# A thirteenth pair of input-projection weight tiles in the block-product stage, and six fewer dense pieces inside attention

## The chip, the cores and the metric

The kernel runs on one core of one Trainium2 chip. The metric is the device time of one execution in microseconds (us), and less is better. The core has five engines that run side by side, each through its own queue in order: PE (TensorE, matmuls and transposes), DVE (VectorE), ACT (ScalarE), POOL (GpSimd) and SP (which here only issues DMAs).

## What is computed

One layer of a hybrid encoder on 1024 prompt rows and 8 x 16 sample rows (1152 rows in all, width 1024). The projection `h @ w_in` has 4352 columns, that is 34 weight tiles of 128 columns, and it is computed for all 1152 rows. Its results feed two attentions, A (8 query heads on 2 key heads) and B (8 heads), and two gates:

```python
h = rmsnorm(x, g_pre_mix)
qa, ka, va, qb, kb, vb, ga, gb = project(h, w_in)        # h @ w_in, 34 tiles of 128 columns
oa = band attention of (qa, ka, va), 3 chunks of 64 keys, with sinks and a bias
ob = band attention of (qb, kb, vb), 9 chunks of 64 keys, with a bias
merged = sigmoid(ga) * (oa @ w_oa) + sigmoid(gb) * (ob @ w_ob)
x = x + rmsnorm(merged @ w_out, g_post_mix)
x = x + rmsnorm(conv_ffn(rmsnorm(x, g_pre_ffn)), g_post_ffn)
```

Every float32 product is made of three fp32r products (high part by high part, high by low, low by high).

## The kernel before

The work runs in stages: normalisation and block products of the input projection, attention, the output projections with the gates, the gated MLP, the down projection. The change touches the first two.

**Block products (lines 160 to 522).** The contraction is halved, the rows are halved, and two weight tiles (a "pair", list `pairs`, line 199) are done together as a 2 x 2 block product in seven products instead of eight. A product is 24 matmuls (4 k-tiles, 3 part products, two chunks of 256 and 320 columns; `chunk_product`, line 136). The first `NA` = 7 pairs have their first two products done early, while the right-hand factors are still being built (`Away`), and the remaining five products later (`head_back`, `tail`). The pairs from the eighth on do all seven in one go (`head`, `tail`). The result goes to DRAM (`in_dr`, one buffer for each weight tile).

**Attention (lines 524 to 914).** Eight units, each of two heads: units 0 to 3 are branch A, 4 to 7 are branch B. A unit has five steps: two prompt steps `p0`, `p1`, the sample step `s`, and `p2`, `p3`. A prompt step handles 256 query rows. It makes scores on PE into the pool `pss1` (2 tiles of two banks; names `s`, line 693), adds the bias and takes the maximum on DVE (line 696), takes the exponential on ACT (line 701), the reciprocal and the scaling on DVE (lines 714, 718). The next step transposes its result on PE into the pool `pst1` (2 banks; names `pt`, line 735), copies each transposed tile to SBUF (`pk`), in turn on ACT (line 739) and DVE (line 737), and multiplies with the values on PE (`o`, line 750). In branch B a row block sees up to 640 keys, in branch A up to 256. The raw q, k and v rows of a unit are loaded and split into high and low parts ahead of time (`k6h`, `k6l`, `q6h`, `q6l`; lines 587 to 591).

**Dense pieces.** The weight tiles that are in no pair are listed in `dense_tiles` (line 840). Each is done without the block scheme, as three pieces of 24 matmuls over 384 rows (`dense_pieces`, line 554; names `d`, lines 117 to 119). A piece is cut in four quanta of 6 matmuls. `pieces_per_unit` (line 865) says how many pieces each unit takes, and `spread` puts their quanta between the instructions of the unit's steps. They give PE work while DVE and ACT prepare the next transposes. Three pieces of the last tile stay for the end, around the last transposes. Each dense weight tile is split into high and low parts by ACT (line 101) and POOL (line 104).

Within these stages the queues are not fixed by hand: a scheduler places each engine's instructions by their order in the program and by when it takes them to be ready.

Of the kernel before, what the change touches and what calls it, by code (L numbers as in the profile page):

```python
# [52 lines left out]
def encoder_step(ctx, tc, x, w_in, w_o, w_out, w_upg, w_down, kc, vc, state_conv, conv_w, conv_b,  # L53
# [109 lines left out]
    with ExitStack() as ph:  # L163
# [32 lines left out]

        pairs = [(4, 5), (0, 1), (2, 3), (10, 14), (6, 7), (11, 15)] + [(18 + n, 26 + n) for n in range(6)]
        NA = 7  # L200
        a1_dr = [dram.tile([P, 2 * CW], F32, name=f"a1_dr{f}") for f in range(NA)]
        rf = {}
# [316 lines left out]
    with ExitStack() as ph:  # L519
# [112 lines left out]
        def fetch(u):  # L632

            un = units[u]
            if u < 4:
                if u == 0:
                    rows(4, "ka", k_done(shared_a, "a", ka_new, 896))
                rows(u, f"q{u}", q_done(un, u))
            else:
                p = u - 4  # L640
                rows(10 + p, f"k{u}", k_done(un, f"{u}", kb_new[p], 512))
                rows(6 + p, f"q{u}", q_done(un, u))
                rows(14 + p, f"v{u}", v_done(un, f"{u}", vb_new[p], 512))
# [193 lines left out]
            later.append(late)  # L837

        later = []
        dense_tiles = [12, 16, 8, 13, 17, 9, 24, 32, 25, 33]  # L840
        pieces = []
        for col in dense_tiles:
            pieces += dense_pieces(col)
# [18 lines left out]
                done = upto  # L862

        fetch(0)
        pieces_per_unit = [3, 3, 3, 3, 4, 4, 4, 3]
        prev = None
        for u in range(8):
            n = pieces_per_unit[u]
# [440 lines left out]
    with ExitStack() as ph:  # L1309
# [119 lines left out]
        def stepper(name, pairs, main, extra, start, extra_start, own=False):  # L1429

            ops = [p.operands(name, own) for p in pairs]
            side = {"p2": "s2", "p1": "s1", "p5": "s1", "p3": "s2"}.get(name)
            n = 2 * len(pairs)

            def step(i, j):
                p, (z, w) = pairs[i // 2], ops[i // 2]
                if j < 0:
                    three(extra, getattr(p, side), w, i % 2, slice(0, P), extra_start and i == 0, i == n - 1)
                else:
                    three(main[j], z, w, i % 2, slice(j * P, (j + 1) * P), start and i == 0, i == n - 1)  # L1440

            return step, n, ([-1] if side else []) + [0, 1, 2, 3]
# [50 lines left out]
        for g in range(2):  # L1493
            last = g == 1
            pairs = [Pair(g, q) for q in range(3)]
# [37 lines left out]
            p5, n, _ = stepper("p5", pairs, xb, ex, False, True)  # L1533
# [4 lines left out]
            p3, n, _ = stepper("p3", pairs, xb, ex, False, False, True)  # L1538
# [94 lines left out]
```

## Time and profile before

| | us |
|---|---|
| median of three runs | 1635.86 (1635.2 to 1637.76) |
| profiled execution | 1635.94 |
| its span, first to last instruction | 1634.1 |
| five full block heads, 185.20 to 296.26 | 111.06 |
| unit 4 (4 pieces) | 44.60 |
| unit 5 (4 pieces) | 43.08 |
| unit 6 (4 pieces) | 43.06 |
| unit 7 (3 pieces) | 38.14 |

1.84 us of the profiled execution lie outside its span. In a timeline, a row is: start, duration, engine, line, operation, output<-inputs, tile, count of merged instructions, and in brackets how long the engine stood idle before it and whom it waited for. In a table of stretches, each engine has its busy time and in parentheses its instructions; PEclk is the granted PE clock as a share of full speed.

### The profile page before, as it was taken

What the parts mean: (1) busy time and instruction counts of PE and PEld (TensorE: products, weight loads), DVE (VectorE), ACT (ScalarE), POOL (GpSimd) and SP (SyncE); (2) the same over time, 40 slices, a digit from 0 to 9 for tenths busy, and PEclk for the clock granted to TensorE, in tenths of its full rate; (3) what the DMA queues carried; (4) which work ended last, traced back from release to release, by engine and by line L of the source; (5) the groups of instructions that cost most, each with busy time, mean ns of one, the idle gap of its engine ahead of it and who ended that gap; (6) DMA issues with size and microseconds to landing.
All of it is one profiled execution on the core that took longest, in us unless ns stands there. A gap on an engine that the chain in (4) does not pass through costs nothing.

```text
span 1634.1 us, 27922 instructions
## 1 busy us (share of the span) xinstructions
PE 1593.4 (98%) x10891; PEld 1470.7 (90%) x10891; DVE 1099.4 (67%) x2045; ACT 728.7 (45%) x1429; POOL 212.1 (13%) x287
## 2 busy tenths in 40 slices
PE   8999999999999999999999999999999999999998
PEld 6999999878788889978899999999999998888886
DVE  6976544777676746444497866766666767955997
ACT  7521233566555444332374344444444445434252
POOL 1000000221110004410002212211112211000002
PEclk9999999999999999999999999999999999999999
DMA  7654321654443255342264321221221219053023
GB/s 282 205 183 150 111 103 67 222 174 152 152 157 102 67 184 195 119 161 90 78 189 136 117 80 57 82 81 67 82 69 67 81 49 367 1 204 124 1 78 154
DMA packets 93045, 205.94 MB, mean 126 GB/s; under 512 B 19321, under 2 KB 42793, under 8 KB 92914
## 3 DMA queue, kind: packets, MB, share of 16 engines
q1 hardware_dynamic: 92640, 203.35, 36.2%
q8 instruction: 85, 1.39, 0.4%
q0 software_dynamic: 272, 0.81, 0.1%
q14 instruction: 46, 0.38, 0.1%
q10 hardware_dynamic: 2, 0.00, 0.0%
HBM read 147.61 MB, written 61.24 MB: 128 GB/s over the span
## 4 chain that ended last, share of the span: by engine, by line
PE 86%; DVE 5%; ACT 3%; DMA 3%; issue 2%; POOL 1%; SPq 0%; DVEq 0%; POOLq 0%; ACTq 0%
PE x L143 16%; PE z L143 8%; PE x L1415 8%; PE ix L143 7%; PE p L1415 6%; PE iz L143 4%; PE y L143 4%; PE o L750 2%; PE d L117 2%; PE pt L735 2%; PE d L119 2%; PE r L1090 2%; PE mp L956 2%; PE mp L958 2%; PE mp L957 2%; PE d L118 2%
## 5 line engine op out<-in xcount | busy, mean ns | idle before, releaser
L143 PE MATMUL x<-xot,s 128*128 128x288 f32 x1152 | 157.7, 295 | 1.5 <-DVE w L1200 1.5
L143 PEld LDWEIGHTS x<-xot,s 128*128 128x128 f32 x1152 | 154.9, 188 | 1.7 <-ACT a L1049 1.7
L1415 PE MATMUL x<-wbp,zap 128*128 128x512 f32 x576 | 135.3, 389 | 0.0
L1415 PEld LDWEIGHTS x<-wbp,zap 128*128 128x128 f32 x576 | 108.1, 188 | 22.5
L1049 ACT ACTIVATE s<-uw 128x512 fp32r<-128x512 f32 x96 | 60.2, 627 | 94.8 <-issue 41.7
L1415 PE MATMUL p<-wbp,zap 128*128 128x512 f32 x432 | 100.5, 389 | 0.0
L701 ACT ACTIVATE p<-p,m 128x256 f32<-128x256 f32 (+4 forms) x128 | 74.8, 587 | 57.3 <-DVE m L696 57.2
L1415 PEld LDWEIGHTS p<-wbp,zap 128*128 128x128 f32 x432 | 81.1, 188 | 16.9
L1050 DVE TENSOR_TENSOR s<-uw,s 128x512 fp32r<-128x512 f32 x96 | 70.2, 731 | 33.8 <-ACT s L1049 33.7
L1241 DVE SCALAR_TENSOR_TENSOR wk<-w,cw,wk 128x128 f32<-128x128 f32 (+2 forms) x144 | 83.2, 614 | 6.7 <-ACT wk L1239 5.9
L1050 DVE TENSOR_TENSOR a<-uw,a 128x512 fp32r<-128x512 f32 x62 | 42.9, 693 | 63.4 <-ACT a L1049 62.2
L143 PE MATMUL x<-xob,s 128*128 128x288 f32 x576 | 81.1, 295 | 3.3 <-DVE wk L1200 3.3
L143 PEld LDWEIGHTS x<-xob,s 128*128 128x128 f32 x576 | 78.1, 188 | 3.9 <-ACT wk L1239 3.1
L143 PE MATMUL z<-xot,s 128*128 128x288 f32 x576 | 80.7, 295 | 0.0
L143 PE MATMUL z<-xot,a 128*128 128x288 f32 x576 | 80.7, 295 | 0.0
L143 PE MATMUL ix<-t,s_i 128*128 128x256 f32 (+1 forms) x576 | 78.4, 294 | 0.7 <-DVE iu L191 0.7
L143 PEld LDWEIGHTS z<-xot,s 128*128 128x128 f32 x576 | 78.1, 188 | 0.0
L143 PEld LDWEIGHTS z<-xot,a 128*128 128x128 f32 x576 | 78.1, 188 | 0.0
L143 PEld LDWEIGHTS ix<-t,s_i 128*128 128x128 f32 x576 | 76.8, 187 | 0.9 <-DVE iu L191 0.9
L176 ACT ACTIVATE s_i<-iw 128x512 fp32r<-128x512 f32 x48 | 30.1, 631 | 86.2 <-PE ix L143 38.1
L143 PE MATMUL x<-xob,a 128*128 128x288 f32 x456 | 63.9, 295 | 0.0
L143 PE MATMUL y<-xob,a 128*128 128x288 f32 x456 | 63.9, 295 | 0.0
(634 smaller groups left out, 3837.1 us busy)
## 6 DMA issues: line engine op xcount, KB each, us to landing
uw<-in_w_upg SPq DMA_DIRECT2D x53, 512.0 KB, 3.7
iw<-in_w_in SPq DMA_DIRECT2D x24, 512.0 KB, 3.7
gg<-in_dr SPq DMA_DIRECT2D x16, 576.0 KB, 4.1
z_dr<-wk SPq DMA_DIRECT2D x23, 256.0 KB, 2.1
in_dr<-gt SPq DMA_DIRECT2D x30, 192.0 KB, 1.9
z_dr<-wk SPq DMA_DIRECT2D x23, 224.0 KB, 1.9
xt<-in_x SPq DMA_DIRECT2D x9, 512.0 KB, 7.6
oT<-o_dr SPq DMA_DIRECT2D x8, 576.0 KB, 6.5
```

What stands on the lines that cost most here:

```text
L117: nc.tensor.matmul(ps, w[:, 0, a], xg[0][:, b], start=start and k == 0, stop=False)
L118: nc.tensor.matmul(ps, w[:, 0, a], xg[1][:, b], start=False, stop=False)
L119: nc.tensor.matmul(ps, w[:, 1, a], xg[0][:, b], start=False, stop=stop and k == nk - 1)
L143: nc.tensor.matmul(ps, w[:, i, k], right(j, c, k), start=first and n == 0, stop=last and n == len(todo) - 1, skip_group_check=True)
L701: nc.scalar.activation(p[h][:, 0:n], p[h][:, 0:n], AF.Exp, bias=least[h], scale=-1.0, accum_out=st.d[:, h, i:i + 1])
L735: nc.tensor.transpose(pt[:, h * nb + b], st.p[i][h][:, c:c + P], ident[:])
L750: nc.tensor.matmul(ps[r, c], k.vs[:, kb, r], p[h], start=n == 0, stop=n == len(st.pv) - 1)
L956: nc.tensor.matmul(ps[:], self.sp[:, 0, k], oT[k][:, 0, c], start=k % 4 == 0, stop=False)
L1049: nc.scalar.activation(sp[:, 0], src, AF.Copy)
L1050: nc.vector.tensor_tensor(sp[:, 1], src, fr(sp[:, 0]), op=ALU.subtract)
L1241: nc.vector.scalar_tensor_tensor(out, src(t), cw[:, f, t:t + 1], out, op0=ALU.mult, op1=ALU.add)
L1415: nc.tensor.matmul(ps, z[:, i, k, c], w[:, j, k], start=first and n == 0, stop=last and n == 2, skip_group_check=True)
```

## The change

Weight tiles 8 and 9 (the queries of units 6 and 7) leave the dense list and become the seventh pair. `NA` stays 7, so the pair (18, 26), which was the seventh, is now the first that does all its products in one go. The list of dense tiles goes from ten to eight, 30 pieces to 24, and the units' shares are set anew: the units of branch A keep three each, those of branch B go from 4, 4, 4, 3 to 2, 3, 2, 2, and three are left for the end as before.

```diff
-        pairs = [(4, 5), (0, 1), (2, 3), (10, 14), (6, 7), (11, 15)] + [(18 + n, 26 + n) for n in range(6)]
+        pairs = [(4, 5), (0, 1), (2, 3), (10, 14), (6, 7), (11, 15), (8, 9)] + [(18 + n, 26 + n) for n in range(6)]
...
-        dense_tiles = [12, 16, 8, 13, 17, 9, 24, 32, 25, 33]
+        dense_tiles = [12, 16, 13, 17, 24, 32, 25, 33]
...
-        pieces_per_unit = [3, 3, 3, 3, 4, 4, 4, 3]
+        pieces_per_unit = [3, 3, 3, 3, 2, 3, 2, 2]
```

On PE, at the end of the block products, before (x, y and z are the accumulators of a pair; `t_` and `xk_` are right-hand factors; each row is the 12 matmuls of one chunk; `w12s` is the first dense tile):

```order
L143 MATMUL ix_0_2964<-xk_129,s_i_3124 128x256 x12
L143 MATMUL ix_1_2965<-xk_129,s_i_3124 128x320 x12
L143 MATMUL iz_0_3028<-t_1038,a_i_3155 128x256 x12
L143 MATMUL iz_1_3029<-t_1038,a_i_3155 128x320 x12
L117 MATMUL d_0_3318<-xk_128,w12s 128x384
```

And after the change, from the same `iz_1_3029` on:

```order
L143 MATMUL iz_1_3029<-t_1038,a_i_3155 128x320 x12
L143 MATMUL ix_0_3188<-xk_128,a_i_3190 128x256 x12
L143 MATMUL ix_1_3189<-xk_128,a_i_3190 128x320 x12
L143 MATMUL iy_0_3220<-xk_129,a_i_3222 128x256 x12
L143 MATMUL iy_1_3221<-xk_129,a_i_3222 128x320 x12
L143 MATMUL iz_0_3252<-t_615,s_i_3255 128x256 x12
L143 MATMUL iz_1_3253<-t_615,s_i_3255 128x320 x12
L143 MATMUL ix_0_3188<-t_616,s_i_3283 128x256 x12
L143 MATMUL ix_1_3189<-t_616,s_i_3283 128x320 x12
L143 MATMUL ix_0_3188<-t_617,s_i_3314 128x256 x12
L143 MATMUL ix_1_3189<-t_617,s_i_3314 128x320 x12
```

Two more products (four rows) follow these before the first dense piece: one more full head stands at the end of the stage.

On PE in step p2 of unit 6, between the first and the second half of the scores, before (`ts` are the transposes of the sample step, `w32s` a dense tile):

```order
L807 MATMUL ts_6544<-ident,pm_3241 128x128
L806 MATMUL ts_6544<-ident,ps_6445 128x128
L807 MATMUL ts_6544<-ident,pm_3245 128x128
L117 MATMUL d_1_6551<-xk_128,w32s 128x384
L118 MATMUL d_1_6551<-xk_128,w32s 128x384
L119 MATMUL d_1_6551<-xk_128,w32s 128x384
```

And after:

```order
L807 MATMUL ts_6646<-ident,pm_3465 128x128
L806 MATMUL ts_6646<-ident,ps_6553 128x128
L807 MATMUL ts_6646<-ident,pm_3469 128x128
L693 MATMUL s_2_1_0_6655<-k6h,q6h 128x320 x2
L693 MATMUL s_2_1_0_6655<-k6h,q6l 128x320 x2
L693 MATMUL s_2_1_0_6655<-k6l,q6h 128x320 x2
L693 MATMUL s_2_1_1_6664<-k6h,q6h 128x320 x2
```

The quantum of six dense matmuls that stood between the two halves is gone, so the second half's scores follow at once; the twelve after the scores remain of eighteen.

On DVE at the end of unit 4, before (`m` and `p` of line 696 are the maxima and sums of the last scores, `k6l` and `q6l` the low parts of unit 6's rows, `oos` the sample output, `oo` the copy of the values' product):

```order
L696 ISA p_3_1_1_5521,m_3_5456<-s_3_1_1_5531,bt_1_5048,m_3_5456 128x320
L589 TENSOR_TENSOR k6l<-k6raw,k6h 128x512 x2
L737 COPY pk_2_5_5559<-pt_2_5_5558 128x256
L714 RECIPROCAL dn_3_5457<-dn_3_5457 128x4
L718 TENSOR_SCALAR p_3_0_0_5458<-p_3_0_0_5458,dn_3_5457 128x640
```

And after:

```order
L696 ISA p_3_1_1_5690,m_3_5637<-s_3_1_1_5700,bt_1_5272,m_3_5637 128x320
L589 TENSOR_TENSOR k6l<-k6raw,k6h 128x512 x2
L591 SCALAR_TENSOR_TENSOR q6l<-q6raw,q6h 128x512
L714 RECIPROCAL dn_3_5638<-dn_3_5638 128x4
L737 COPY pk_2_5_5728<-pt_2_5_5727 128x256
L718 TENSOR_SCALAR p_3_0_0_5639<-p_3_0_0_5639,dn_3_5638 128x640
```

One of the two halves of the split `q6l` now stands ahead of the reciprocal and the scaling of the last step; before, both stood behind them.

## The prediction

> **What bounds the kernel now.** I read the page first, then PE's timeline and the table of stretches for the two stages that the change touches, then DVE's timeline inside attention. From the page, the span, PE's busy time, and the chain of work that ended last, by engine:
>
> ```profile
> span 1634.1 us, 27922 instructions
> PE 1593.4 (98%) x10891; PEld 1470.7 (90%) x10891; DVE 1099.4 (67%) x2045; ACT 728.7 (45%) x1429; POOL 212.1 (13%) x287
> PE 86%; DVE 5%; ACT 3%; DMA 3%; issue 2%; POOL 1%; SPq 0%; DVEq 0%; POOLq 0%; ACTq 0%
> ```
>
> PE is the bound nearly everywhere: work taken from it counts, as long as it doesn't then stand waiting. Stretches of time (length, then busy time and instruction count of PE, PEld, DVE, ACT, POOL, then PE's clock and the DMA): the last five heads of the block products, unit 0, and units 4 to 7.
>
> ```profile
> 185.20:296.30 111.10, 111.10 (x843) 111.10 (x842) 47.47 (x82) 38.71 (x78) 7.83 (x16) 1.00 0.31 105
> 296.30:323.00 26.70, 25.89 (x221) 20.95 (x221) 21.49 (x80) 15.95 (x56) 2.40 (x5) 1.00 0.59 191
> ...
> 411.83:456.43 44.60, 41.61 (x346) 34.74 (x344) 33.28 (x104) 23.95 (x59) 7.54 (x9) 0.96 0.52 165
> 456.43:499.51 43.08, 42.80 (x370) 35.66 (x368) 30.75 (x104) 23.32 (x58) 5.60 (x8) 1.00 0.43 144
> 499.51:542.57 43.06, 42.78 (x371) 35.65 (x369) 28.80 (x100) 22.07 (x55) 3.20 (x2) 1.00 0.25 82
> 542.57:580.71 38.14, 37.94 (x337) 30.30 (x335) 27.88 (x99) 19.87 (x51) 1.72 (x1) 1.00 0.17 54
> ```
>
> In the heads PE has no gap and DVE is busy 43%. In units 5 to 7 PE has almost no gap either, but there that is the work of the dense pieces: DVE is already at 67% to 73%, and what PE does between two dense quanta waits on DVE and ACT.
>
> **The change, part by part.**
>
> *The added head.* The first product of a head starts at 185.20, the first of the next at 207.41, and the first dense matmul after five heads at 296.26:
>
> ```profile
> 185.20 3.33 PE L143 MATMUL ix<-xk,a_i 128*128 128x256 f32 x24
> 207.41 3.33 PE L143 MATMUL ix<-xk,a_i 128*128 128x256 f32 x24
> ...
> 296.26 0.34 PE L117 MATMUL d<-xk,w12s 128*128 128x384 f32 x1
> ```
>
> 111.06 / 5 = 22.21 us per head. Nothing hides an extra one, since PE has no gap there; it also loads two weight tiles and stores four results, beside DMA at 0.31 of its time. That (18, 26) loses its early start and (8, 9) gains it leaves seven early pairs. **+22.2.**
>
> *The six dense pieces.* Inside one piece:
>
> ```profile
> 580.99 0.34 PE L118 MATMUL d<-xk,w33s 128*128 128x384 f32 x1
> ...
> 584.98 1.03 PE L735 MATMUL pt<-ident,p 128*128 128x128 f32 x8
> ```
>
> 23 matmuls take 3.99 us, 0.1735 each, so a piece of 24 is 4.16 and six are 25.0: two from unit 4, one from unit 5, two from unit 6, one from unit 7. **-25.0** of PE work. The two weight splits and six copies to SBUF that go with them lay on ACT and POOL, beside PE: I count them as nothing.
>
> Without any new wait the sum is 22.2 - 25.0 = -2.8. What decides is how much of the 25.0 comes back as PE waiting in units 4 to 7.
>
> *The first piece taken from a unit* is in the trace already: unit 6 has four pieces and lasts 43.06, unit 7 three and 38.14. Unit 6 has also the transposes of unit 7's values:
>
> ```profile
> 513.96 0.66 PE L621 MATMUL vt<-ident,v7raw 128*128 128x128 f32 x4
> 514.88 0.66 PE L621 MATMUL vt<-ident,v7raw 128*128 128x128 f32 x4
> ```
>
> 43.06 - 38.14 - 1.32 = 3.6, so a piece of 4.16 bought 3.6, and 0.56 came back.
>
> *The second piece* isn't in the trace. The chains that it uncovers are, in unit 6. DVE after the first scores of p2, after the last, and in p3; PE at the start of each group of scores:
>
> ```profile
> 522.79 0.41 PE L693 MATMUL s<-k6h,q6h 64*128 64x320 f32 x2
> 525.51 0.42 PE L693 MATMUL s<-k6h,q6h 64*128 64x320 f32 x2
> 526.34 0.31 PE L693 MATMUL s<-k6l,q6h 64*128 64x320 f32 x2
> 530.93 0.42 PE L693 MATMUL s<-k6h,q6h 64*128 64x320 f32 x2
> ```
>
> ```profile
> 525.31 0.08 DVE L696 DVE_READ_ACCUMULATOR2_ANT m<- 128x1 f32 x1
> ...
> 528.19 0.09 DVE L696 DVE_READ_ACCUMULATOR2_ANT m<- 128x1 f32 x1
> 529.61 0.18 DVE L714 RECIPROCAL dn<-dn 128x4 f32<-128x4 f32 x1 [1.33 <-ACT p L701]
> 529.82 1.94 DVE L718 TENSOR_SCALAR p<-p,dn 128x640 f32<-128x640 f32 x4
> 531.69 0.49 DVE L696 CUSTOM_DVE_ANT_0 p<-s,bt 128x320 f32<-128x320 f32 x1
> ...
> 533.46 0.69 DVE L737 COPY pk<-pt 128x512 f32<-128x512 f32 x1
> ```
>
> (1) Scores have two tiles. DVE frees the second at 525.39, and PE wants it after 525.51: covered by one quantum (6 x 0.1735 = 1.04), which the change takes out there. PE would want it at about 524.9: a wait of 0.5. (2) From the end of the scores (526.65) to the end of the scaling (531.76) are 5.1 us, in which PE has dense work, the sample step's values and the next scores (530.93, about 1.1 long): 5.4 of cover. A quantum less leaves 4.35: a wait of 0.75. (3) In p3 the fourth transposed tile waits for DVE's copy of the second, which stands behind four maxima, until 533.46 + 0.69; PE had a quantum there, now none: about 0.5. Together 1.75 for a second piece; in p0 and p1 the copies and exponentials pace PE too, but the scheduler moved the next scores forward into those gaps, and I add nothing for them.
>
> *The splits on DVE.* One half of `q6l` now stands ahead of the last scaling of unit 4. Both halves of such a split take 1.29:
>
> ```profile
> 498.63 1.29 DVE L591 SCALAR_TENSOR_TENSOR q7l<-q7raw,q7h 128x512 fp32r<-128x512 f32 x2
> ```
>
> so half is 0.65, and the transposes of unit 5's p0, queued on PE behind that scaling, come later by it: 0.65.
>
> Returned: unit 4 0.56 + 1.75 = 2.3, unit 5 0.56, unit 6 2.3, unit 7 (its second piece) 1.75, the split 0.65: 7.6. **Sum: 22.2 - 25.0 + 7.6 = +4.8.** The profiled execution took 1635.94, and the median of the runs is 1635.86, so no correction is due: **1640.7 us.**
>
> Bounds of the returned time. Below: 0, all waits covered. Above, by how densely DVE is seen to work: its 33.28 + 30.75 + 28.80 + 27.88 = 120.7 us in units 4 to 7 fill 168.9. In unit 7 it is busy 0.731 of the time; no denser, the four units would still last 165.1, only 3.8 would be saved, and the sum is +18.4. In unit 0 it is 21.49 / 26.70 = 0.805; at that the units last 149.9, 19.0 are saved, and the sum is +3.2. In both rows PE was the bound, so neither is a limit of DVE; the denser one is the nearer, and it lies by my sum.
>
> **The rivals.**
>
> *A: the cover holds.* The scheduler moved scores forward, and ACT is busy only half of these units. With under 5 us returned, 3 say, the time is 1635.9 - 2.8 + 3 = 1636.1: no difference. Against it: unit 7 returned 0.56 for its one piece.
>
> *B: faster, by the pause of unit 4.* In p0 of unit 4 PE stands still for 2.39 + 0.59, and its clock falls after that:
>
> ```profile
> 412.92 3.48 DVE L591 SCALAR_TENSOR_TENSOR q5l<-q5raw,q5h 128x512 fp32r<-128x512 f32 x2
> 413.18 2.67 POOL L104 TENSOR_TENSOR w9s<-w9r,w9s 128x1024 fp32r<-128x1024 f32 x1 [1.37 <-issue]
> 417.90 0.44 PE L735 MATMUL pt<-ident,p 128*128 128x128 f32 x2 [2.39 <-DVE pk L737]
> 419.10 1.54 PE L750 MATMUL o<-pk,vsa 128*64 128x256 f32 x12 [0.59 <-ACT pk L739]
> ...
> 418.00:420.00 2.00, 1.41 (x12) 1.02 (x14) 1.19 (x5) 1.32 (x5) 0.00 (x0) 0.90 0.92 280
> 420.00:422.00 2.00, 2.00 (x15) 1.67 (x14) 0.48 (x2) 0.00 (x0) 0.00 (x0) 0.50 1.00 396
> 422.00:424.00 2.00, 2.00 (x14) 1.28 (x13) 1.79 (x7) 1.40 (x5) 0.00 (x0) 0.75 0.63 233
> ```
>
> The split of q5 took 3.48 instead of 1.29 while POOL split tile 9. The lost clock is 0.1 x 2 + 0.5 x 2 + 0.25 x 2 = 1.7, the pause 3.0. Tile 9 leaves. If nothing took its place the whole 4.7 would go, and with no more than 4 returned elsewhere the time would be below 1632.6. It decides if POOL is idle while DVE splits q5. Against it: in the changed queues POOL splits tile 32 at the same place, behind the same four memsets, and ACT's half of that split follows the same `q5h`. The Trainium skill, SBUF — State Buffer, section on the two separate sides, says that a DVE operation with two SBUF inputs and a GpSimd operation lock each other out of a shared port pair for a whole instruction; the trace agrees (3.48 against 1.29), and by that the pause comes again whichever tile is split.
>
> *C: much slower, PE's clock.* The pause of unit 4 cost 1.7 in clock. If the new waits come close enough together in three places to do the same, that is 5.1 and some 1.5 of longer waits: 14.2 returned, +11.4, 1647.3. For it: one such place is seen. Against it: the waits worked out are 0.5 to 0.75, with work between them. The Trainium skill, TensorE: Matmul & The Clock Gate, Part 1, has the clock halved only after an idle window of about 3.4 us; the fall here, after 2.39 and 0.59 with work between, is near that, and by the rule C would lose its price but for the waits.
>
> **How the numbers follow.** A measurement of this kernel can tell about 0.2% (3.3 us) from no change. My forecast, 5 to 10 us returned (+2.2 to +7.2): 0.48, two thirds of it slower by over 0.2%. A: 0.22, within. B: 0.09, faster. C and other ways to more than 10: 0.21, slower. So faster 0.09, within 0.2% 0.36, slower 0.55. The range reaches from just under the sum without waits (1633.2) to C's price: 1632.5 to 1647.5, leaving out most of B and the loose end of the DVE bound (+18.4), whose row has PE as its bound.
>
> **What would show it.** Right: attention begins 22.2 later (at 318.5), ends about 17.4 sooner after its start, and units 4 to 7 last about 38.6, 40.1, 37.0 and 35.7 with PE's idle rows ahead of `s`, `pt` and `o` adding up to some 8 us, released by DVE and ACT. The pause of unit 4 stands beside POOL's split of tile 32. Wrong: a head that costs less than 22, units 4 to 7 shorter by 22 or more together, no pause in unit 4, or a PE clock below 0.9 in several places of attention.

## The result: 9.9 us slower, and the profile after

| | time (us) | against before |
|---|---|---|
| before | 1633.17, median of 6 (1630.32 to 1637.76) | |
| after | 1643.02, median of 6 (1641.35 to 1644.87) | 1.0062, 95% interval 1.005 to 1.0075 |
| forecast | 1640.7 (1632.5 to 1647.5) | +4.8 |

The change is slower, by 9.9 where 4.8 was forecast. The profiled execution of after took 1644.87 (span 1643.0), 8.9 above that of before. Its page, busy times and the chain that ended last:

```profile
span 1643.0 us, 28005 instructions
...
PE 1598.6 (97%) x10915; PEld 1469.7 (89%) x10915; DVE 1106.3 (67%) x2062; ACT 731.4 (45%) x1436; POOL 205.5 (13%) x285
...
PE 84%; DVE 6%; ACT 4%; DMA 3%; issue 2%; POOL 0%; SPq 0%; DVEq 0%; POOLq 0%; ACTq 0%
```

PE was to do 2.8 less and shows 5.2 more. In units 4 to 7 its busy time fell by 16.1 (165.1 to 149.0) where 25.0 of work left. So some 8.9 of lost time stand inside the busy time, and the page hides them: 1.7 is clock (below), and the rest is waiting inside the rows of queued matmuls, which shows in the waits of the weight loads (PEld, further down). The timeline of after, first product of the late heads and first dense matmul:

```profile
186.42 3.33 PE L143 MATMUL ix<-xk,a_i 128*128 128x256 f32 x24
...
319.70 0.34 PE L117 MATMUL d<-xk,w12s 128*128 128x384 f32 x1
```

133.28 is six heads of 22.21, one more than before. (The heads begin 1.2 later than before; PE's instructions up to there are the same in both programs, and in all the runs of twelve or thirteen pairs below it lay between 183.2 and 188.3.) Units 4 to 7, cut where the output of p2 ends; length, busy time and count of PE, PEld, DVE, ACT, POOL, then PE's clock and the DMA:

```profile
435.50:475.20 39.70, 36.31 (x294) 27.57 (x294) 32.31 (x104) 22.11 (x56) 5.50 (x9) 0.91 0.50 157
475.20:516.90 41.70, 40.94 (x354) 32.11 (x348) 30.43 (x104) 22.65 (x57) 4.76 (x8) 1.00 0.46 140
516.90:555.00 38.10, 36.88 (x323) 27.87 (x321) 29.13 (x101) 20.68 (x52) 2.37 (x1) 1.00 0.28 91
555.00:590.50 35.50, 34.89 (x313) 26.99 (x311) 28.16 (x99) 19.52 (x50) 0.00 (x0) 1.00 0.12 37
```

Against 44.60, 43.08, 43.06 and 38.14 that is 4.9, 1.4, 5.0 and 2.6 less; with the tail of unit 7, up to the first matmul behind attention, 14.4 in all (from 189.35 to 174.95). 25.0 of work left, so 10.6 came back as waiting and lost clock. Behind attention both traces take the same time (1032.9 and 1032.5).

The pause of unit 4 is there, beside POOL's split of tile 32. DVE, POOL and PE in after:

```profile
436.62 3.46 DVE L591 SCALAR_TENSOR_TENSOR q5l<-q5raw,q5h 128x512 fp32r<-128x512 f32 x2
...
436.87 2.65 POOL L104 TENSOR_TENSOR w32s<-w32r,w32s 128x1024 fp32r<-128x1024 f32 x1 [1.37 <-issue]
...
440.55 0.69 PE L693 MATMUL s<-k4h,q4h 64*128 64x384 f32 x2 [2.23 <-DVE m L696]
```

and the clock around it (the column behind POOL's):

```profile
440.00:442.00 2.00, 1.45 (x6) 1.02 (x7) 1.52 (x10) 1.62 (x7) 0.00 (x0) 0.57 0.76 206
442.00:444.00 2.00, 1.72 (x10) 0.94 (x11) 1.19 (x5) 0.99 (x4) 0.00 (x0) 0.50 0.90 305
444.00:446.00 2.00, 2.00 (x14) 1.59 (x11) 1.02 (x4) 0.00 (x0) 0.00 (x0) 0.50 0.80 321
446.00:448.00 2.00, 2.00 (x12) 1.43 (x10) 1.76 (x7) 1.74 (x5) 0.00 (x0) 0.72 0.64 246
```

2 x (0.43 + 0.5 + 0.5 + 0.28) = 3.4 of clock, where before lost 1.7; PE's idle time there is less, 2.23 and 0.28 against 2.39 and 0.59.

### The profile page after: what moved, and what is told of

It is laid out like the page before. It is cut to its first block, busy times and chain, and to the rows that moved or that the text cites. A ratio compares the mean times of both kernels' runs of the same rounds, so it can differ in the third digit from the quotient of the medians.

```text
span 1643.0 us, 28005 instructions
## 1 busy us (share of the span) xinstructions
PE 1598.6 (97%) x10915; PEld 1469.7 (89%) x10915; DVE 1106.3 (67%) x2062; ACT 731.4 (45%) x1436; POOL 205.5 (13%) x285
## 4 chain that ended last, share of the span: by engine, by line
PE 84%; DVE 6%; ACT 4%; DMA 3%; issue 2%; POOL 0%; SPq 0%; DVEq 0%; POOLq 0%; ACTq 0%
PE x L143 16%; PE z L143 8%; PE ix L143 8%; PE x L1415 8%; PE p L1415 6%; PE iz L143 4%; PE y L143 4%; PE mp L956 2%; PE mp L957 2%; PE r L1091 2%; PE mp L958 2%; PE r L1092 2%; PE r L1090 2%; PE o L750 2%; PE pt L735 2%
## 5 line engine op out<-in xcount | busy, mean ns | idle before, releaser
L1415 PEld LDWEIGHTS p<-wbp,zap 128*128 128x128 f32 x432 | 81.1, 188 | 16.9
L143 PE MATMUL ix<-t,s_i 128*128 128x256 f32 (+1 forms) x624 | 84.9, 294 | 1.3 <-DVE iu L191 1.3
L143 PEld LDWEIGHTS ix<-t,s_i 128*128 128x128 f32 x624 | 83.1, 187 | 1.5 <-DVE iu L191 1.5
```

Of the source, the lines that this page charges most:

```text
L143: nc.tensor.matmul(ps, w[:, i, k], right(j, c, k), start=first and n == 0, stop=last and n == len(todo) - 1, skip_group_check=True)
L1415: nc.tensor.matmul(ps, z[:, i, k, c], w[:, j, k], start=first and n == 0, stop=last and n == 2, skip_group_check=True)
```

## Experiments

Theories at the start. **1**: dense pieces had covered waits in units 4 to 7, and the thin fill uncovers them. **2**: the early side costs more than its 22.2. **3**: only the pause of unit 4 and the clock behind it matter. "Units 4 to 7" below is the stretch from unit 4's first score to the first matmul behind attention, read from each run's windows.

### One part at a time

*The thin fill alone* (on before; unit 3 takes one piece more, for tile 9's due time):

```diff
-        pieces_per_unit = [3, 3, 3, 3, 4, 4, 4, 3]
+        pieces_per_unit = [3, 3, 3, 4, 2, 3, 2, 2]
```

> The kernel before, computing the same, with only the dense pieces per unit changed: 3, 3, 3, 4, 2, 3, 2, 2 and eight at the end (before: 3, 3, 3, 3, 4, 4, 4, 3 and three). No extra pair, so TensorE's work is that of before; the fill of units 4 to 7 is that of after (unit 3 takes one piece more, which the due time of tile 9 asks for). Theory 1 (the thin fill uncovers waits, some 10.6 in after, of which about 1.8 is a longer clock loss in the pause of unit 4): units 4 to 7 give back 6 x 4.16 = 25.0 less some 9, the end takes 5 x 4.16 = 20.8 more and unit 3 4.2 more; before + 9 if the pause of unit 4 is there as before. GpSimd's split of tile 9 now stands one piece earlier, ahead of four small memsets: if it no longer falls beside the split of q5, the pause of 3.0 and its clock loss of 1.7 go and before + 4. Theory 2 (the waits are what the prediction said, 7.6, and what was missed lies ahead of attention): 3 less than Theory 1, before + 6, or + 1 to + 2 without the pause. Theory 3 (only the pause of unit 4 and the clock after it matter): without the pause, faster than before by 3 to 5.

Measured: 1645.83 against 1633.34, ratio 1.0077 (1.0063 to 1.0091): slower by 12.5, more than any theory gave, and with the pause of unit 4 gone. The direction is Theory 1's. Theory 3 had it 3 to 5 faster and falls here, and again below, where neither kernel has a pause. Three losses are this edit's own. POOL, DVE and PE at the start of unit 5:

```profile
450.02 2.37 POOL L104 TENSOR_TENSOR w24s<-w24r,w24s 128x1024 fp32r<-128x1024 f32 x1
...
450.38 2.56 DVE L591 SCALAR_TENSOR_TENSOR q6l<-q6raw,q6h 128x512 fp32r<-128x512 f32 x1
...
453.44 0.66 PE L735 MATMUL pt<-ident,p 128*128 128x128 f32 x4 [1.39 <-DVE oo L752]
```

Half a split takes 0.68 elsewhere; here 2.56, until 0.55 past POOL's end with tile 24: unit 4's pause has come up in unit 5. And in unit 6 `q7raw` came late, since tile 9 was now only just done. ACT, then PE:

```profile
501.80 1.15 ACT L587 ACTIVATE q7h<-q7raw 128x512 fp32r<-128x512 f32 x2 [3.72 <-DMA q7raw<-in_dr]
...
504.27 0.44 PE L735 MATMUL pt<-ident,p 128*128 128x128 f32 x2 [1.61 <-DVE oo L752]
```

DVE's split of q7 waits for ACT's half, `oo` stands behind that split, and PE behind `oo`. The third is in the sample step of unit 7: DVE's four scalings into `pm` (line 798) take 2.96 beside POOL's split of tile 25, where the four before them took 0.94; PE waits 0.85 and 1.07, and loses 1.7 of clock. Together the three are 6.6 in the profiled execution. That execution is the shortest of the five (1642.35), with 9.2 more in attention than before; what else is in the median's 12.5 was not traced.

*The extra head alone* (on after, the old fill put back):

```diff
-        dense_tiles = [12, 16, 13, 17, 24, 32, 25, 33]
+        dense_tiles = [12, 16, 13, 13, 17, 17, 24, 32, 25, 33]
...
-        pieces_per_unit = [3, 3, 3, 3, 2, 3, 2, 2]
+        pieces_per_unit = [3, 3, 3, 3, 4, 4, 4, 3]
```

> After with the pair of tiles 8 and 9 still made in the head, but with the old fill of attention: pieces 3, 3, 3, 3, 4, 4, 4, 3 and three at the end, where tiles 13 and 17 are done twice (the second time the same values are written again) in place of tiles 8 and 9. So it is the extra head alone, with TensorE's work 22.2 above before. Theories 1 and 3: before + 22.2, that is 1655.4 where before is 1633.2, and units 4 to 7 as long as in before (29.5, 44.6, 43.1, 43.1, 38.1 by the old boundaries). Theory 2 (the early side costs more than its instructions): before + 23.4 or more, with attention's first dense matmul 23.4 later as in the profiled after.

Measured: 1656.39, ratio 1.0146 (1.013 to 1.0162), +23.1. The interval, 21.2 to 26.5, holds both 22.2 and 23.4, so the times don't settle Theory 2. In the trace, from the first late product (188.31) to the first dense matmul (321.58) are again 133.27, so the heads cost no more than 22.2 each. What lies ahead of them varies: the late heads begin at 183.5 to 188.3 in the six kept traces of thirteen pairs and at 183.2 to 187.4 in the seven of twelve, on average 0.7 later. That is within the scatter: Theory 2 is not borne out, but an early side that is dearer by 1 or so is not excluded. The pause of unit 4 in this run, PE and then the clock:

```profile
442.93 0.44 PE L735 MATMUL pt<-ident,p 128*128 128x128 f32 x2 [2.40 <-DVE pk L737]
...
444.12 1.09 PE L750 MATMUL o<-pk,vsa 128*64 128x256 f32 x12 [0.59 <-ACT pk L739]
```

```profile
443.00:445.00 2.00, 1.41 (x15) 0.98 (x15) 1.19 (x5) 1.34 (x6) 0.00 (x0) 1.00 0.91 344
445.00:447.00 2.00, 2.00 (x20) 1.45 (x17) 1.45 (x6) 0.36 (x1) 0.00 (x0) 1.00 0.99 337
```

The same 2.40 and 0.59, and no clock lost.

*Unit 4's pause taken out*, in after and, in the same way for tile 9, in before:

```diff
-                    box["w"] = weight_tile(w_in[col], f"w{col}")
+                    box["w"] = weight_tile(w_in[col], f"w{col}", "scalar", "vector" if col == 32 else "gpsimd")
```

> After, computing the same, with the low half of tile 32's split (one subtraction of 128x1024) on VectorE in place of GpSimd, so that nothing of GpSimd lies beside the split of q5. Theory 1: the split of q5 takes 1.3 instead of 3.46, the pause of unit 4 (TensorE busy 2.82 of 4.50 and then 3.17 of 4.00: 2.5 idle) and the clock loss after it (0.57, 0.50, 0.50, 0.50, 0.72 over five slices: about 3.4 to 4) go: after - 5 to - 6, so still 3 to 5 above before. Theory 3: the same, but then level with before. Against both: the subtraction on VectorE takes some 1 to 2.5, stands close behind the split of q5 and ahead of maxima, and may hold the scores up by as much: after - 3.

> Before, computing the same, with the low half of tile 9's split on VectorE in place of GpSimd. The split of q5 in unit 4 took 3.48 beside it and 1.29 elsewhere. Theories 1 and 3: the pause of unit 4 (3.0) and the lost clock (1.7) go: before - 3 to - 4.7, about 1629. Rival: VectorE is filled as before, the subtraction takes the time of what it frees, and scores wait for maxima instead: before - 0 to - 1.

Measured: after so 1639.13, ratio to before 1.0039 (1.0027 to 1.0052), 3.9 less than after; before so 1630.43, ratio 0.9986 (0.9976 to 0.9996), 2.9 less than before. DVE and PE in the thin one:

```profile
434.55 1.28 DVE L591 SCALAR_TENSOR_TENSOR q5l<-q5raw,q5h 128x512 fp32r<-128x512 f32 x2
...
436.86 1.22 DVE L104 TENSOR_TENSOR w32s<-w32r,w32s 128x1024 fp32r<-128x1024 f32 x1
...
438.53 0.44 PE L735 MATMUL pt<-ident,p 128*128 128x128 f32 x2 [1.43 <-ACT pk L739]
```

The split takes 1.28 with POOL idle, so POOL's work beside it was the cause. (The Trainium skill, SBUF — State Buffer, section on the two separate sides, says so of DVE and GpSimd; the runs agree: 3.46 and 2.56 beside POOL's split, 1.28 and 0.68 without.) What is late next is a transposed tile, 1.43. The pause was worth 3.5 in units 4 to 7 of after (174.95 to 171.49) and 3.4 in before's (189.35 to 185.96): the same, whatever the clock did, so it is no part of the difference. These two are the base for the rest:

```profile
410.25:596.21 185.96, 181.34 (x1529) 151.25 (x1527) 124.02 (x412) 94.16 (x232) 15.20 (x19) 1.00 0.36 117
```

```profile
433.45:604.94 171.49, 163.49 (x1386) 128.03 (x1384) 123.16 (x413) 90.06 (x224) 10.17 (x16) 1.00 0.37 114
```

First the full, then the thin fill: 14.5 saved, 10.5 of 25.0 returned, with no pause in either.

### How much a piece covers

*One piece less in each unit*, on the pause-free before:

```diff
-        pieces_per_unit = [3, 3, 3, 3, 4, 4, 4, 3]
+        pieces_per_unit = [3, 3, 3, 3, 3, 3, 3, 2]
```

> The kernel before with tile 9's low half split on VectorE (as the run e4_before_nolock, 1630.4), computing the same, with dense pieces 3, 3, 3, 3, 3, 3, 3, 2 and seven at the end: one piece less in each of units 4 to 7, none in a second. TensorE's work unchanged. As the prediction priced it (a unit's first piece costs 0.56, its second 1.75): 4 x 0.56, so e4 + 2.2 to + 3, about 1633. Theory 1 as the traces have it since (10.6 returned for six pieces: 1.8 a piece, the first as dear as the second): 4 x 1.8, e4 + 7, about 1637.5.

Measured: 1637.16 against 1633.59, ratio 1.0019 (1.0007 to 1.0031); against the base's 0.9986 that is 5.4, and 5.8 in the traces. (By the prediction's own count unit 7's piece was already a second one, so its price is 3.4, not 2.2.) Units 4 to 6 of this run:

```profile
412.84:451.50 38.66, 37.17 (x323) 29.73 (x321) 31.01 (x104) 23.34 (x58) 2.02 (x5) 1.00 0.54 160
451.50:492.90 41.40, 40.31 (x347) 31.68 (x345) 30.46 (x103) 21.74 (x55) 5.01 (x7) 1.00 0.40 130
492.90:535.20 42.30, 39.88 (x345) 31.39 (x343) 29.60 (x101) 21.80 (x55) 3.47 (x6) 1.00 0.32 105
```

and of the base:

```profile
410.25:451.49 41.24, 39.99 (x346) 33.69 (x344) 31.93 (x105) 23.90 (x59) 4.97 (x9) 1.00 0.57 179
451.49:494.60 43.11, 42.83 (x371) 35.69 (x369) 30.79 (x104) 23.29 (x58) 5.30 (x8) 1.00 0.43 145
494.60:537.65 43.05, 42.78 (x371) 35.65 (x369) 28.75 (x100) 22.06 (x55) 3.23 (x2) 1.00 0.25 81
```

A first piece of 4.16 saves 2.6, 1.7 and 0.75, and returns 1.6, 2.5 and 3.4; 1.6 of the last is PE's wait in unit 6 behind the late `q7raw`, as in the thin fill alone. So about 1.6 to 2.5 where the prediction had 0.56. Unit 7 with one piece less and the end with four more took 1.6 less than their work. With three pieces at the end, as in the base, PE stands idle for 2.62 ahead of the first matmul behind attention, until ACT has copied the first rows of the attention's output; here it does not wait at all. So four units returned 8.4, 1.0 of it in unit 7, and the 5.4 is what is left after the longer end has filled that gap.

*The opposite: a pair less in the head, six pieces more in attention*, on the same base:

```diff
-        pairs = [(4, 5), (0, 1), (2, 3), (10, 14), (6, 7), (11, 15)] + [(18 + n, 26 + n) for n in range(6)]
+        pairs = [(4, 5), (0, 1), (2, 3), (10, 14), (6, 7)] + [(18 + n, 26 + n) for n in range(6)]
...
-        dense_tiles = [12, 16, 8, 13, 17, 9, 24, 32, 25, 33]
+        dense_tiles = [11, 15, 12, 16, 8, 13, 17, 9, 24, 32, 25, 33]
...
-        pieces_per_unit = [3, 3, 3, 3, 4, 4, 4, 3]
+        pieces_per_unit = [4, 4, 4, 4, 5, 4, 4, 4]
```

> The opposite of the change, on the base of e4_before_nolock and computing the same: the pair of tiles 11 and 15 is taken out of the head as well (eleven pairs), its two tiles become six dense pieces, first in the row, and the fill is 4, 4, 4, 4, 5, 4, 4, 4 and three at the end, one piece more in units 0 to 4 and 7. TensorE's work - 22.2 + 25.0 = + 2.8. If a denser fill covers no more waits: e4 + 2.8, about 1633. Theory 1 (pieces cover waits for VectorE and ScalarE that are still there: in e4's trace TensorE stands idle for 4.4 in units 0 to 3 and for 1.2 in unit 4, with as much again inside matmul rows): 3 to 6 covered, e4 - 0 to - 3, about 1629.

Measured: 1633.32, ratio 0.9992 (0.9979 to 1.0006): above the base by 2.9 in the medians of two sessions and by 1.0 in the ratios, each to the before of its own session. PE is busy 1592.3 against 1589.5, the 2.8 of work. The whole times can't tell whether waits were covered, but the traces can. From the first score of unit 0 to that of unit 4, four pieces more (16.6) make 127.36 out of 113.94, so 3.2 were covered. In units 4 and 7 a piece more makes 44.85 out of 41.24 and 61.79 out of 58.56 (unit 7 with its tail), which covers 0.55 and 0.9. But unit 5, with no piece more, lasts 46.41 instead of 43.11. DVE, POOL and PE there:

```profile
449.99 3.46 DVE L591 SCALAR_TENSOR_TENSOR q6l<-q6raw,q6h 128x512 fp32r<-128x512 f32 x2
...
450.27 2.63 POOL L104 TENSOR_TENSOR w24s<-w24r,w24s 128x1024 fp32r<-128x1024 f32 x1 [0.52 <-POOL bt L660]
...
453.96 0.65 PE L735 MATMUL pt<-ident,p 128*128 128x128 f32 x4 [1.56 <-DVE oo L752]
```

The pause is back, beside tile 24's split. PE stands 1.56, and the clock falls to 0.77, 0.50 and 0.87 in the three slices of 2 us from 454, 1.7 lost: together the 3.3 of unit 5. So some 4.7 were covered, as Theory 1 guessed (3 to 6), and this edit's pause took 3.3 of it back. A piece more still covers 0.5 to 0.9 each, against 1.6 to 2.5 that one less returns; without the pause this version was not run.

### What PE waits for

*The scaling left out in units 4 to 7*, under the thin and the full fill:

```diff
-                for h in range(2):
+                for h in range(2 if u < 4 else 0):
                     nc.vector.tensor_scalar(st.p[i][h][:, 0:n], st.p[i][h][:, 0:n], st.d[:, h, i:i + 1], None,
```

> The run e3_nolock (after with tile 32's low half split on VectorE, 1639.1) with the scaling of the probabilities by their sums left out in units 4 to 7 (sixteen scalings, some 6.4 of VectorE's time in each of these units; their numbers are then not normalized). If VectorE is what the thinned units wait for: the returned waits of 10.6 go almost whole, e3 - 7 to - 9, and with e8 the thin fill then costs nothing: e7 = e8 - 2.8 to + 1. Rival (the waits are for ScalarE's copies of transposed tiles, or TensorE's own changes of operation): e3 - 0 to - 3, and e7 = e8 + 5 or more.

> The run e4_before_nolock (before with tile 9's low half split on VectorE, 1630.4) with the same scalings left out in units 4 to 7. Under the full fill few waits for VectorE are left there (in the trace of e4 some 1 to 1.5 in each unit): e4 - 1 to - 4 by both theories; it is the base for e7.

Measured: thin 1636.68, ratio 1.0012 (1.0001 to 1.0023); full 1630.24, ratio 0.9973 (0.9961 to 0.9984). The thin fill is still 6.4 slower than the full one, of 8.7 with the scaling. Their windows, thin, then full:

```profile
435.89:603.47 167.58, 160.59 (x1385) 127.94 (x1384) 99.16 (x348) 89.00 (x224) 8.53 (x16) 1.00 0.36 117
```

```profile
414.24:598.71 184.47, 180.07 (x1529) 151.27 (x1527) 99.69 (x349) 94.08 (x232) 13.37 (x18) 1.00 0.37 118
```

DVE does 24 less in either. 16.9 saved, 8.1 returned, where it was 10.5: VectorE's load carries 2.4 of the returned time, not most of it. That part of Theory 1 falls.

*Three PSUM rooms for transposed tiles and outputs, one for dense pieces*, in place of two and two (a room is one buffer of the pools `pst1` and `psd1`). Theory 4 is that a transposed tile waits until the one two before it has been copied out of its room. Run on both bases and on the thin one without scaling:

```diff
-        psd = ph.enter_context(tc.tile_pool(name="psd1", bufs=2, space=PSUM, reuse_waits="tile"))
+        psd = ph.enter_context(tc.tile_pool(name="psd1", bufs=1, space=PSUM, reuse_waits="tile"))
...
-        pst = ph.enter_context(tc.tile_pool(name="pst1", bufs=2, space=PSUM, reuse_waits="tile"))
+        pst = ph.enter_context(tc.tile_pool(name="pst1", bufs=3, space=PSUM, reuse_waits="tile"))
```

> The run e3_nolock (after, tile 32's low half split on VectorE; 1639.1), computing the same, with three rooms in place of two for transposed tiles and outputs in PSUM, and one in place of two for dense pieces. Theory 1 fell as far as VectorE's load goes: without the scaling (6.4 us a unit) the thin fill still cost 7 more than the full one. Theory 4: most of the returned waits are a transposed tile or an output that waits until ScalarE or VectorE has copied the one two before it, which dense matmuls between them hid; a third room takes that wait away: e3 - 4 to - 6, and 4 to 5 above e10. Rival, Theory 5 (what is returned is spread over the chain from scores by maxima, exponentials and scaling to transposes, whatever the rooms): e3 - 1 to + 1. Against both: with one room a dense piece must wait until ScalarE has copied the piece before, up to 0.6 at each of 21 pieces, at most 10.

> The run e4_before_nolock (before, tile 9's low half split on VectorE; 1630.4), computing the same, with the same rooms: three for transposed tiles and outputs, one for dense pieces. By Theory 4 little is left to take away under the full fill in units 4 to 7 (some 1 to 1.5 each) and 4.4 in units 0 to 3: e4 - 2 to - 4. By Theory 5: e4 - 1 to + 1. With dense pieces held up by their single room: e4 + 2 to + 10.

> The run e7_thin_noscale (after, tile 32's low half split on VectorE, the scaling of the probabilities left out in units 4 to 7; 1636.7) with the same rooms: three for transposed tiles and outputs, one for dense pieces. If the waits for VectorE and the waits for rooms are two parts of the returned time that add up (Theory 4): e7 - 4 to - 6, then within 3 of e8_full_noscale. By Theory 5: e7 - 1 to + 1.

Measured, against a before of 1634.35: thin 1638.90, ratio 1.0025 (1.0011 to 1.004); full 1634.33, ratio 1.0003 (0.9991 to 1.0014); thin without scaling 1633.62, ratio 0.9996 (0.9986 to 1.0006). In whole times that is no clear gain for the thin fill, a loss for the full one, and 2.6 (by the ratios) instead of the expected 4 to 6 for the thin one without scaling. But it is two effects. Units 4 to 7 of the thin one and of the full one:

```profile
436.86:602.65 165.79, 157.64 (x1386) 128.01 (x1384) 121.66 (x414) 88.29 (x224) 10.15 (x18) 1.00 0.37 118
```

```profile
416.82:600.88 184.06, 180.17 (x1529) 152.03 (x1527) 123.23 (x414) 93.25 (x232) 15.29 (x19) 1.00 0.37 118
```

5.7 shorter than its base under the thin fill, 1.9 under the full one: Theory 4 holds there, and of 25.0 now 6.7 is returned. (The 3.8 between them is the most that the rooms carry: PEld waits 1.5 for the single dense room under the full fill and 0.6 under the thin one, so up to 0.9 of it may be that.) Units 0 to 3 became longer, from 112.65 to 118.13 under the thin fill and from 113.94 to 118.32 under the full one. That dense pieces wait for their single room shows as 1.1 of PEld's waits there; the rest of those 4.4 and 5.5 was not traced. Without the scaling as well, the thin fill's stretch is

```profile
438.10:599.46 161.36, 155.63 (x1385) 127.10 (x1383) 98.81 (x350) 87.91 (x224) 8.58 (x16) 1.00 0.38 121
```

10.1 below its base: the two parts add up (5.7 + 3.9). If the full fill's own gains (1.9 and 1.5) added up likewise, 3.8 would still be returned; a full fill with both was not run.

PEld's waits from unit 4's first score to the end of unit 7's p2 (sum, times, longest) show the same two parts, the pause-free before first,

```profile
PEld pt L735 <- ACT pk L739: 3.4, 5, 1.6
...
PEld s L693 <- DVE m L696: 1.0, 4, 0.2
```

then the pause-free after,

```profile
PEld pt L735 <- ACT pk L739: 5.8, 13, 1.7
...
PEld s L693 <- DVE m L696: 4.0, 12, 0.5
...
PEld o L750 <- DVE pk L737: 1.8, 3, 0.7
```

and the thin fill with three rooms:

```profile
PEld pt L735 <- ACT pk L739: 4.1, 5, 1.6
...
PEld s L693 <- DVE m L696: 2.4, 7, 0.5
```

Scores wait for maxima 12 times instead of 4 (0.33 each), transposed tiles for ACT's copies 13 times instead of 5 (0.45 each). With the third room the copies are waited for 5 times again, for 4.1 in place of 5.8, and the scores 7 times; that they gain because they stand behind those tiles in PE's queue is likely, not shown.

### A version that beats both

*The third room only from unit 4 on*, under the full fill without the pause:

```diff
-        psd = ph.enter_context(tc.tile_pool(name="psd1", bufs=2, space=PSUM, reuse_waits="tile"))
+        psd = ph.enter_context(tc.tile_pool(name="psd1", bufs=1, space=PSUM, reuse_waits="tile"))
+        psx = ph.enter_context(tc.tile_pool(name="psx1", bufs=1, space=PSUM, reuse_waits="tile"))
...
+        def dense_room(name):
+            room["d"] += 1
+            if room["late"] or room["d"] % 2:
+                return psd.tile([P, GW], F32, name=name, tag="d")
+            return psx.tile([P, 512], F32, name=name, tag="x")[:, 0:GW]
+
+        def tr_room(name):
+            if room["late"]:
+                room["t"] += 1
+                if room["t"] % 3 == 0:
+                    return psx.tile([P, 512], F32, name=name, tag="x")
+            return pst.tile([P, 512], F32, name=name, tag="pt")
...
+            room["late"] = u >= 4
```

> The run e4_before_nolock (before, tile 9's low half split on VectorE; before - 2.9), computing the same, with one PSUM room that changes hands: in units 0 to 3 dense pieces take turns in it and in one of their own, as before two, and from unit 4 on every third transposed tile or output goes there. With three rooms throughout (e10) units 0 to 3 became 4.4 longer, which is dense pieces waiting for their single room, and units 4 to 7 1.9 shorter (184.1 against 186.0 from unit 4's first score to the first matmul behind attention). If both are read rightly: units 0 to 3 as in e4, units 4 to 7 1.9 shorter, e4 - 1 to - 2, before - 4 to - 5, about 1629. If the change of hands costs a wait of its own, or the single dense room holds pieces up in units 4 to 7 too: e4 - 0 to + 2.

Measured: 1630.87 against 1634.34, ratio 0.998 (0.9968 to 0.9992). Units 4 to 7:

```profile
411.50:597.77 186.27, 181.70 (x1529) 152.45 (x1527) 123.56 (x412) 93.39 (x232) 15.64 (x18) 1.00 0.36 117
```

As long as the base's 185.96, and units 0 to 3 (113.74) too. The 1.9 did not come. 1.0 of it is one wait of PE at 416.57, at the start of unit 4, for ACT's copy of a transposed tile, which the full fill with three rooms throughout does not have; the rest is open. It and its base are both a little faster than before, 0.998 and 0.9986, and not told apart; the base, one argument changed in before, is the one to take.

## Why the prediction was right, and what it had too small

- *The extra head, +22.2, nothing hides it*: right; six heads in 133.28, and +23.1 by itself.
- *Six pieces, -25.0 of PE work*: right; the opposite change moved PE's busy time by the 2.8 of the sum.
- *The pause of unit 4 comes again, beside tile 32*: right, against rival B. Its price of 4.7 was too high: 3.4 or 3.5 in the traces, 2.9 and 3.9 in the medians, since a transposed tile is late next.
- *The second piece of a unit, 1.75*: about right. Units 4 and 6 returned 3.4 each for two pieces. Less the firsts as measured (1.6; 3.4 - 1.6 for the late `q7raw`) that leaves 1.8 and 1.6. The agreement is partly luck: the three waits that it was added up from were not found one by one, and waits are in other steps too (below).
- *The first piece, 0.56*: this term was mis-sized. The prediction took it from unit 6 less unit 7; with one piece taken from each unit it returned 1.6 to 2.5. In its own windows unit 7 had less to do on ACT (19.87 against 22.07) and on DVE (27.88 against 28.80), which may be why it showed too little; that was not tried. Unit 5, which gave up one piece only, shows it best: 2.8 where 0.56 + 0.65 was forecast. With the first piece at 2.5, as with one piece taken from each unit, 0.3 is left for the split of `q6l`, forecast at 0.65; no run tries that by itself.
- *Unit 7, 1.75*: 1.1, counted with its tail (58.6 to 55.5), and 1.0 with one piece taken from each unit; too much.
- Sum of what returned: 10.6 for 7.6. The forecast of +4.8 becomes +7.8; the profiled executions differ by 8.9, 1.2 of it ahead of the late heads, and the medians by 9.9 (8.2 to 12.2). The 2 that are left of the medians have no term and stay open. What returned lies outside the 5 to 10 that had the largest chance, among the ways to more than 10 that had 0.21. The direction came from the right mechanism. That the time is within the range is partly luck: the upper end stood at the price of Rival C, the clock, and what was larger were the waits. (The shares of the chances add up to 0.38 within and 0.53 slower, where 0.36 and 0.55 stand.)
- *Where it waits*: the places were right in kind (scores for maxima, transposed tiles for copies, the chain through the scaling), but in the thin one without the pause scores wait for maxima 12 times in four units and transposed tiles for copies 13 times, more often than the p2 and p3 of the sum. Of the 10.5, rooms carry at most 3.8 and the scaling 2.4; the rest, some 4, is in neither and stays open.
- *Idle rows of PE of some 8*: not seen so. In units 4 to 7 PE's own waits are 5.5, and were 3.7 before; most of what was added is inside matmul rows and shows only as PEld's waits.
- Rival A, the cover holds: no. Rival C, clock lost in three places: no; only in unit 4.

## What to carry to other kernels

Filler work between dependent steps hides waits, and taking it out saves less than its own time. How much less depends on the fill: here a piece of 4.16 taken out returned 1.6 to 2.5, a piece put in covered 0.5 to 0.9. So price a removed piece by taking one piece out and running it, since the nearest pair of units gave about a third of the price or less. Count waits on the weight loads' row as well as on the matmuls', since a queued matmul that waits is counted as busy. When a pause comes from two engines at work side by side, look where the pair meets after every change of order: here it moved from unit 4 to unit 5 in two of the experiments, and hid in one of them what the pieces had gained.

## What the runs showed of the hardware

- The same pause on PE (2.39 or 2.40, then 0.59, with work between) cost 1.7 of clock in the profiled execution of before and none with the extra head alone. In after, where the clock had fallen to 0.57 in the slice in which an idle time of 2.23 ended, it cost 3.4. The Trainium skill, TensorE: Matmul & The Clock Gate, Part 1, has a free-running window of about 3.4 us decide; that the same pause costs once and not again agrees with that. That a whole idle window is needed is not what after shows, where no gap next to the fall is longer than 2.23, nor the version with eleven pairs, which lost 1.7 after gaps of 1.56 and 0.66. Single gaps of 1.43 (after without the pause) and 1.57 (one piece less) cost nothing.
- DVE's subtraction of 128x1024 for a weight tile takes 1.22 where POOL's takes 2.37 to 2.65: moving one of them cost DVE little and took 3 to 4 us off.
- A split on DVE met by POOL's split ends only after it: half a split took 2.56 instead of 0.68, a whole one 3.46 to 3.48 instead of 1.28.
